# The first norm's rows stored unscaled, and scaled for the residual in the mLSTM, a block of rows at a time

## The chip, the cores and the metric

The kernel runs on one core of a Trainium2 chip. A core has five engines with instruction queues of their own, which meet only at semaphores: TensorE (PE in the profile, its weight loads PEld), VectorE (DVE), ScalarE (ACT), GpSimd (POOL) and SyncE (SP), which here only issues transfers. Each engine takes its instructions strictly in the order of its row. The metric is the device time of one execution in microseconds (us).

## The reference, cut

One layer of a decoder over 1024 tokens of width 1024:

```python
x = layer_norm(x, ln_in_g, ln_in_b)
h = x @ w_in                      # 7888 columns: gated DeltaNet, mLSTM, latent attention, gates
y_gdn, y_mlstm, y_mla = gated_deltanet(...), mlstm(...), latent_attention(...)
merged = sum(sigmoid(gate_b) * (y_b @ P_b) for b in branches)
x = layer_norm(ALPHA * x + merged @ w_out, ln1_g, ln1_b)      # ALPHA = 2 ** 0.25
x = layer_norm(ALPHA * x + routed_experts(x), ln2_g, ln2_b)
```

The change is about the term `ALPHA * x` of the second norm. With `xn` for the first norm's rows before their gain and shift, it is `xn * (ALPHA * ln_in_g) + ALPHA * ln_in_b`, row by row, 1024 rows of 1024 values.

## The kernel before

The 1024 rows are 8 blocks (`NB`) of 128 rows, a row to a partition. `input_norm` loads the rows into two tiles `xh` (four blocks each), normalises them in place on ScalarE and turns them through PE into `xH` and `xL`, the high and low part of x, with the gain and the shift put in on the way. So `xh` itself holds the rows without gain and shift. From then on PE works through `w_in` in chunks of 256 columns (tiles `wr` as loaded, `wh` and `wl` split). The first six wide chunks feed the convolutions of the gated DeltaNet: a product `psp`, its copy `ci` by ScalarE (`conv_half`, L519, after a small `memset` on GpSimd, L514), four taps `cy` on VectorE (L531, L533), a tanh on ScalarE, and `cth` to memory as `gqkv`. Beside them run the `gates_prep` steps (`da` on GpSimd, `c_mprev`, `c_mt` on VectorE, `c_emt` on ScalarE).

At the end of that stage `residual()` (L257) stores the residual: it zeroes one spare block of rows (`zr` to `x1r`), loads ALPHA times gain and shift into every partition (`gr`, `br`, L317, scaled on GpSimd in L319), and for each of the 8 blocks multiplies and adds on GpSimd (L265, L266) and stores `x0a` from GpSimd's own queue (L267). `out_proj` reads `x0a` much later.

PE's instruction order is written by hand for the whole front half. Independent products (`Filler`) are handed out in small pieces between dependent steps; the numbers `MRATE` and `MFILL` set how much of them stands between two steps. In the first stage GpSimd's order is by hand too; in the mLSTM the order on GpSimd, VectorE, ScalarE and SyncE is the scheduler's, but it is fixed at compile time.

The mLSTM (`mlstm`, L994) goes through the 8 blocks. `mlstm_prep` of block b+1 runs with `mlstm_main` of block b. A block's chain is: loads `mx`, `mv`, `mo_`; `mR` and its split on GpSimd and ScalarE (L914 to L919); PE's `mpk`, `mps`, `mpD`; an exponential into `mE` on ScalarE, masked on GpSimd (L931); `mkw`, `ms`, `mkk`, `mqd` on VectorE (L933 to L945); PE's `mpn` and `mpc`; on VectorE the denominators `mnn`, whose power of -1/2 is taken on GpSimd (L132, called from `rsqrt`); GpSimd scales `mo_` with it (L983); VectorE multiplies `mso` (L985); PE turns it (`mpy`), ScalarE copies it to `myT`, and SyncE stores it to `ym`. Meanwhile PE's filler computes the branch gates (`gt`, stored to `gates`).

Of the kernel before, what the change touches and what calls it, by code (L numbers as in the profile page):

```python
# [19 lines left out]
P = 128  # L20
# [124 lines left out]
class Filler:  # L145
    """Work for the tensor engine that waits for nothing, handed out in small pieces between dependent steps."""

# [27 lines left out]
def drive(k, us, *gens):  # L175
    """Steps the generators in turn, with filler after each step."""
    live = list(gens)
    while live:
        for g in list(live):
            try:  # L180
                n = next(g)
            except StopIteration:
                live.remove(g)
                continue
            k.fill.run(us * (n or 1.0))
# [8 lines left out]
def input_norm(k, late, todo, conv):  # L194
    """The first norm, a half of the rows at a time: while the first half is turned, the second is normalised. The
    tensor engine follows with the narrow columns of w_in, and the first wide ones' product with the first half."""
    nc, tc = k.nc, k.tc
# [59 lines left out]
    def residual():  # L257
        z = pool.tile([P, D], F32, name="zr", bufs=1)
        nc.gpsimd.memset(z, 0.0)
        nc.gpsimd.dma_start(k.x1r[T:T + P, :], z)  # L260
        gr = bcast_row(k, pool, k.ln_in_g, "gr", ALPHA)
        br = bcast_row(k, pool, k.ln_in_b, "br", ALPHA)
        for b in range(NB):
            xa = xh[b // 4][:, b % 4, :]
            nc.gpsimd.tensor_tensor(xa, xa, gr, OP.mult)  # L265
            nc.gpsimd.tensor_tensor(xa, xa, br, OP.add)  # L266
            nc.gpsimd.dma_start(k.x0a[b * P:(b + 1) * P, :], xa)  # L267

# [54 lines left out]
def load_raw(k, pool, src, segs, width, kt=KD, ncols=D_IN, tag="w", bufs=2, pieces=2, rtag=None, rbufs=2, rpool=None,  # L323
             now=False):
    """Loads a weight in pieces of its rows."""
    wh = pool.tile([P, kt, width], F32R, name=tag + "h", tag=tag + "h", bufs=bufs)
    wl = pool.tile([P, kt, width], F32R, name=tag + "l", tag=tag + "l", bufs=bufs)
    step = max(1, kt // pieces)

    def parts():  # L330
        for a in range(0, kt, step):
            n = min(step, kt - a)
            raw = (rpool or pool).tile([P, step, width], F32, name=tag + "r", tag=rtag or tag + "r", bufs=rbufs)
            o = 0
            for start, m in segs:
                ap = bass.AP(tensor=src.tensor, offset=src.offset + a * P * ncols + start,
                             ap=[[ncols, P], [P * ncols, n], [1, m]])
                k.nc.sync.dma_start(raw[:, :n, o:o + m], ap)
                o += m
            s = slice(a, a + n)  # L340
            yield raw[:, :n, :o], wh[:, s, :o], wl[:, s, :o]

    return wh, wl, list(parts()) if now else parts()


def split_raw(k, w):
    """Splits what was loaded into a high and a low part."""
    wh, wl, parts = w
    for raw, h, l in parts:
        k.nc.scalar.activation(h, raw, AF.Copy)  # L350
        k.nc.vector.tensor_sub(l, raw, h)  # L351
    return wh, wl
# [42 lines left out]
def chunks(k, todo):  # L395
    """Column chunks of w_in one after the other, each split one chunk ahead of its products."""
    def load(i):
        return load_split(k, k.wp, k.w_in, [(todo[i][0], 256)], 256)

    w = load(0)  # L400
    for i, (_, fn) in enumerate(todo):
        nxt = load(i + 1) if i + 1 < len(todo) else None
        yield from fn(w)
        w = nxt
# [117 lines left out]
def conv_steps(k, pool, t, ci):  # L522
    """The causal convolution of four taps over a row of columns, and its SiLU, operation by operation."""
    nc = k.nc
# [156 lines left out]
def inverse16(k, pool, b):  # L681
    """The 16-row diagonal blocks of the unit triangular inverse, row by row, a block to a partition."""
    nc = k.nc
# [14 lines left out]
    nc.sync.dma_start(blk_diag(k.gTd[b % 2]), X3)  # L698
    nc.sync.dma_start(blk_diag(k.gUd[b % 2]), t)


# [293 lines left out]
def mlstm(k):  # L995
    with k.tc.tile_pool(name="mls", bufs=1, side="right") as pool:
        Cn = pool.tile([P, H, P + 1], F32, name="mC")
        st = {}
        drive(k, k.rate, mlstm_prep(k, pool, 0, st))
        for b in range(NB):  # L1000
            gens = [mlstm_main(k, pool, b, Cn, st)]
            if b + 1 < NB:
                gens.insert(MORD, mlstm_prep(k, pool, b + 1, st))
            drive(k, MRATE, *gens)
            k.fill.run(MFILL)

# [52 lines left out]
def mla_prep(k, keep, lat, pool):  # L1059
    """The rotated keys and the normed latents, transposed."""  # L1060
    nc = k.nc
# [61 lines left out]
def mla(k, wn, wpool, after):  # L1123
    """Attention a head at a time: the scores of the next two blocks of rows go ahead of the values of these."""
    nc = k.nc
# [241 lines left out]
def route_choose(k, pool, lo, hi):  # L1367
    """Scores, choice and weights of the tokens of blocks lo to hi."""
    nc = k.nc
# [21 lines left out]
def route_place(k, pool, lo, hi):  # L1391
    """Places of the tokens of blocks lo to hi in their experts' rows, from 1; 0 where an expert is not chosen."""
    nc = k.nc
# [25 lines left out]
def route_weights(k, pool, lo, hi):  # L1419
    """The weights of the chosen experts, in three parts that add up exactly."""  # L1420
    nc = k.nc
# [22 lines left out]
def places(k, oh, aux, cols=(0, 6), parts=False):  # L1444
    """The rows of an expert's blocks: where to read, where to add, and their weights over the residual's scale. The
    first block has whole rows; of the others, with `parts`, each has 32 rows in quarters, partition 32q + r being
    quarter q of row r."""
    nc = k.nc
# [82 lines left out]
def mm_pair(k, outs, xH, xL, ws, first, last):  # L1531
    """One contraction step of two products that share their left operand."""
    for p in range(3):
# [14 lines left out]
class Weights:  # L1548
    """The experts' weights in the order of their use. A slot holds one as it comes, or the high or the low part of
    one; slots come free in a known order and are handed on in it."""  # L1550

# [44 lines left out]
    def step(self, split=True):  # L1596
        """After a step, the last to use the oldest parts."""
        self.free += self.parts.pop(self.done)[2:]
# [7 lines left out]
    def spare(self, keep=False):  # L1606
        """A slot for other data; with `keep`, one that outlives the experts."""
        i = next((i for i, (p, _) in enumerate(self.free) if p is not self.late), 0)
# [10 lines left out]
    def whole(self, keys):  # L1619
        """The weights as they come; each is asked for once."""  # L1620
        for key in keys:
            self.seen.add(self.index[key])
            yield self.raw[self.index[key]][0]
# [19 lines left out]
def experts(k, ws):  # L1643
    """Per expert a block of 128 rows always, and up to four of 32 rows each where it has more: those take a quarter of
    the columns in each quarter of the tensor engine. The tensor engine and the indirect transfers alone branch on the
    count: what the others read of a skipped product is finite and not added anywhere."""
    nc, tc = k.nc, k.tc
# [41 lines left out]
    with tc.tile_pool(name="moe", bufs=2) as pool:  # L1689
# [103 lines left out]
        def last_two(d, e):  # L1793
            """All but the rows of the last expert's first block goes into the residual first, and the last norm runs
            over all rows; then over those rows again, once they are whole."""
            a, norm = A[e], Norm(k)
# [73 lines left out]
def overflow(k):  # L1870
    """Rows past the first two blocks of an expert, added to the residual row by row, and the last norm over all rows
    again."""
    nc, tc = k.nc, k.tc
# [55 lines left out]
class Norm:  # L1929
    """The last norm: statistics on the scalar engine for some blocks, and the scale and shift on GpSimd for some."""  # L1930

# [25 lines left out]
    def rows(self, alloc):  # L1957
        """All rows, block by block: loads, statistics, scale, and the way out."""
        k, nc = self.k, self.k.nc
# [122 lines left out]
def out_proj(k, mH, mL, w, wA, xpool):  # L2082
    """The merged branches through w_out, a quarter of the columns at a time, and row by row the norm, the logits and
    the routing."""
    nc, tc = k.nc, k.tc
    with tc.tile_pool(name="wop", bufs=2) as pool:
# [63 lines left out]
        def logits(b):  # L2150
            """Four chunks at a time, each in a quarter of the tensor engine's columns."""
            pq = k.pb.tile([P, P], F32, name="plq", tag="t")
# [238 lines left out]
```

## Time and profile before

| what | value |
|---|---|
| median of 3 runs | 1935.11 us (1934.57, 1935.11, 1947.82) |
| span of the profiled execution | 1943.0 us |
| PE busy | 1735.4 us (89%) |
| DVE busy | 1225.7 us (63%) |
| ACT busy | 702.9 us (36%) |
| POOL busy | 601.7 us (31%) |
| mean granted TensorE clock | 0.950 |

The profile is of one execution. Its own time on the device beyond the span is not listed; the span alone lies between the second and the third of the runs. Times in a timeline are counted from the start of the span. A row of a timeline gives start, duration, engine, line, operation, output and inputs; what stands in brackets at the end is the idle time of the engine just before it and what ended that. Busy shares are means over stages that have different limits, so the stages are read one by one: the first norm and the convolutions up to about 220 us, the gated DeltaNet up to about 742, the mLSTM to about 877.

### The profile page before, as it was taken

What the parts mean: (1) busy time and instruction counts of PE and PEld (TensorE: products, weight loads), DVE (VectorE), ACT (ScalarE), POOL (GpSimd) and SP (SyncE); (2) the same over time, 40 slices, a digit from 0 to 9 for tenths busy, and PEclk for the clock granted to TensorE, in tenths of its full rate; (3) what the DMA queues carried; (4) which work ended last, traced back from release to release, by engine and by line L of the source; (5) the groups of instructions that cost most, each with busy time, mean ns of one, the idle gap of its engine ahead of it and who ended that gap; (6) DMA issues with size and microseconds to landing.
All of it is one profiled execution on the core that took longest, in us unless ns stands there. A gap on an engine that the chain in (4) does not pass through costs nothing. (4 is left out here: it accounts for less than half of the span.)

```text
span 1943.0 us, 29520 instructions
## 1 busy us (share of the span) xinstructions
PE 1735.4 (89%) x10830; PEld 1448.4 (75%) x10830; DVE 1225.7 (63%) x2279; ACT 702.9 (36%) x1166; POOL 601.7 (31%) x503
## 2 busy tenths in 40 slices
PE   6996999999999999999999899998488887788772
PEld 5974988899998888888777688897356655566551
DVE  7699654554555424444577657636776778899766
ACT  6311222212112213335344422212335455566453
POOL 3186021113301105531100200015434455455355
PEclk9998999999999999999999999998689998889886
DMA  5232633333332225432200365433557778788645
GB/s 170 88 109 108 186 101 119 96 104 112 102 107 80 94 78 163 137 123 104 62 18 29 124 195 181 163 114 142 209 186 222 236 229 267 233 283 299 206 116 201
DMA packets 210665, 286.42 MB, mean 147 GB/s; under 512 B 33358, under 2 KB 138824, under 8 KB 210472
## 3 DMA queue, kind: packets, MB, share of 16 engines
q1 hardware_dynamic: 202312, 258.87, 40.3%
q0 software_dynamic: 8160, 24.91, 5.4%
q8 instruction: 129, 2.11, 0.4%
q14 instruction: 64, 0.52, 0.1%
HBM read 214.64 MB, written 69.07 MB: 146 GB/s over the span
## 5 line engine op out<-in xcount | busy, mean ns | idle before, releaser
L365 PE MATMUL psp<-xH,wh 128*128 128x512 f32 x704 | 286.4, 407 | 18.0 <-ACT ci L519 18.0
L366 PE MATMUL psp<-xL,wh 128*128 128x512 f32 x704 | 276.0, 392 | 4.2 <-POOL ci L514 2.3
L367 PE MATMUL psp<-xH,wl 128*128 128x512 f32 x704 | 276.9, 393 | 0.0
L365 PEld LDWEIGHTS psp<-xH,wh 128*128 128x128 f32 x704 | 133.3, 189 | 43.7 <-ACT ci L519 19.3
L365 PE MATMUL psp<-wh,xH 128*128 128x256 f32 (+1 forms) x576 | 165.7, 288 | 0.0
L367 PE MATMUL psp<-wh,xL 128*128 128x256 f32 (+1 forms) x576 | 162.4, 282 | 0.0
L366 PE MATMUL psp<-wl,xH 128*128 128x256 f32 (+1 forms) x576 | 162.4, 282 | 0.0
L366 PEld LDWEIGHTS psp<-xL,wh 128*128 128x128 f32 x704 | 133.3, 189 | 31.9 <-POOL ci L514 2.7
L367 PEld LDWEIGHTS psp<-xH,wl 128*128 128x128 f32 x704 | 132.8, 189 | 29.4
L1535 PE MATMUL ph<-wl,xgH 128*128 128x512 f32 x274 | 94.8, 455 | 19.6 <-PEq L1656 8.7
L365 PEld LDWEIGHTS psp<-wh,xH 128*128 128x128 f32 x576 | 110.4, 192 | 0.2
L366 PEld LDWEIGHTS psp<-wl,xH 128*128 128x128 f32 x576 | 110.4, 192 | 0.1
L367 PEld LDWEIGHTS psp<-wh,xL 128*128 128x128 f32 x576 | 110.3, 191 | 0.0
L351 DVE TENSOR_TENSOR wl<-wr,wh 128x1024 fp32r<-128x1024 f32 (+1 forms) x62 | 81.8, 1339 | 41.9 <-ACT wh L350 29.9
L350 ACT ACTIVATE wh<-wr 128x1024 fp32r<-128x1024 f32 (+1 forms) x62 | 64.0, 1048 | 64.6 <-PE psp L366 40.7
L1535 PEld LDWEIGHTS ph<-wl,xgH 128*128 128x128 f32 x274 | 55.5, 215 | 36.5 <-issue 11.5
L365 PE MATMUL pbr<-yH,brh 128*128 128x512 f32 x192 | 76.0, 396 | 0.5 <-DMA brr<-in_w_br_gdn_dram 0.5
L366 PE MATMUL pbr<-yL,brh 128*128 128x512 f32 x192 | 76.4, 398 | 0.0
L367 PE MATMUL pbr<-yH,brl 128*128 128x512 f32 x192 | 76.0, 396 | 0.0
L365 PE MATMUL pwo<-woh,mH 128*128 128x256 f32 x256 | 75.9, 297 | 0.0
L366 PE MATMUL pwo<-wol,mH 128*128 128x256 f32 x256 | 74.3, 290 | 0.0
L367 PE MATMUL pwo<-woh,mL 128*128 128x256 f32 x256 | 74.2, 290 | 0.0
(844 smaller groups left out, 4442.5 us busy)
## 6 DMA issues: line engine op xcount, KB each, us to landing
wl<-in_moe_w_dram SPq DMA_DIRECT2D x126, 256.0 KB
wr<-in_w_in_dram SPq DMA_DIRECT2D x60, 512.0 KB
xs<-in_moe_w_dram SPq DMA_DIRECT2D x82, 256.0 KB
wl<-in_moe_w_dram SPq DMA_DIRECT2D x34, 512.0 KB
gates<-gt SPq DMA_DIRECT2D x24, 512.0 KB
mgt<-gates SPq DMA_DIRECT2D x48, 256.0 KB
we<-in_moe_w_dram SPq DMA_DIRECT2D x48, 256.0 KB
we<-in_moe_w_dram SPq DMA_DIRECT2D x18, 512.0 KB
```

Source lines behind the costliest of these rows:

```text
L350: k.nc.scalar.activation(h, raw, AF.Copy)
L351: k.nc.vector.tensor_sub(l, raw, h)
L365: k.nc.tensor.matmul(out, aH, bH, start=start, stop=False)
L366: k.nc.tensor.matmul(out, aH, bL, start=False, stop=False)
L367: k.nc.tensor.matmul(out, aL, bH, start=False, stop=stop)
L1535: k.nc.tensor.matmul(ps, xL if p == 2 else xH, wl if p == 1 else wh, start=first and p == 0, stop=last and p == 2)
```

## The change

Two parts. In the first stage the rows of `xh` are stored to `x0a` as they are, by SyncE, without any work on GpSimd; the zero rows are stored by SyncE too. In the mLSTM a new class `Residual` loads `gr` and `br` and scales them, and after the steps of each block b its method `block(b)` loads 128 rows of `x0a` into a tile `rx` (two buffers), multiplies and adds on GpSimd, and stores them back to the same place. The other lines of the diff only empty docstrings, so that line numbers move.

```diff
     def residual():
         z = pool.tile([P, D], F32, name="zr", bufs=1)
         nc.gpsimd.memset(z, 0.0)
-        nc.gpsimd.dma_start(k.x1r[T:T + P, :], z)
-        gr = bcast_row(k, pool, k.ln_in_g, "gr", ALPHA)
-        br = bcast_row(k, pool, k.ln_in_b, "br", ALPHA)
+        nc.sync.dma_start(k.x1r[T:T + P, :], z)
         for b in range(NB):
-            xa = xh[b // 4][:, b % 4, :]
-            nc.gpsimd.tensor_tensor(xa, xa, gr, OP.mult)
-            nc.gpsimd.tensor_tensor(xa, xa, br, OP.add)
-            nc.gpsimd.dma_start(k.x0a[b * P:(b + 1) * P, :], xa)
+            nc.sync.dma_start(k.x0a[b * P:(b + 1) * P, :], xh[b // 4][:, b % 4, :])
...
+class Residual:
+
+
+    def __init__(self, k, pool):
+        self.k, self.pool = k, pool
+        self.gr = bcast_row(k, pool, k.ln_in_g, "gr", ALPHA)
+        self.br = bcast_row(k, pool, k.ln_in_b, "br", ALPHA)
+
+    def block(self, b):
+        nc, rows = self.k.nc, self.k.x0a[b * P:(b + 1) * P, :]
+        x = self.pool.tile([P, D], F32, name="rx", bufs=2)
+        nc.sync.dma_start(x, rows)
+        nc.gpsimd.tensor_tensor(x, x, self.gr, OP.mult)
+        nc.gpsimd.tensor_tensor(x, x, self.br, OP.add)
+        nc.sync.dma_start(rows, x)
...
         Cn = pool.tile([P, H, P + 1], F32, name="mC")
+        res = Residual(k, pool)
         st = {}
...
             drive(k, MRATE, *gens)
+            res.block(b)
             k.fill.run(MFILL)
```

PE's and ScalarE's rows keep their order, VectorE's but for one weight split that comes ahead of a `mso`. GpSimd's and SyncE's rows change. In the rows below, numbers behind a name tell buffers apart, and the lines of the changed kernel are its own: L914 to L919 of before are L926 to L931, L931 is L943, L983 is L995.

GpSimd at the start of the mLSTM, before: the second block's addition into `mR` and the first block's `mE` follow each other closely.

```order
L916 TENSOR_TENSOR mR<-mR,mR_6706 128x512
L915 TENSOR_TENSOR mR_6859<-ident,c_nmt 128x512
L931 TENSOR_TENSOR mE<-mE,TU 128x512
L919 TENSOR_TENSOR mRL<-mR,mRH 128x512
L914 TENSOR_TENSOR mR<-TU,c_fp 128x512
```

The same place in the changed kernel:

```order
L928 TENSOR_TENSOR mR<-mR,mR_6690 128x512
L314 TENSOR_SCALAR gr<-gr 128x1024
L927 TENSOR_TENSOR mR_6848<-ident,c_nmt 128x512
L314 TENSOR_SCALAR br<-br 128x1024
L943 TENSOR_TENSOR mE<-mE,TU 128x512
L931 TENSOR_TENSOR mRL<-mR,mRH 128x512
L926 TENSOR_TENSOR mR<-TU,c_fp 128x512
```

The two scalings of gr and br have come ahead of the first `mE`.

GpSimd right behind that, before, down to the first block's `mo_` (`mnn` is the power, L132):

```order
L916 TENSOR_TENSOR mR<-mR,mR_6859 128x512
L915 TENSOR_TENSOR mR_7008<-ident,c_nmt 128x512
L908 MEMSET mv_6853 128x4
L132 TENSOR_TENSOR mnn<-mnn,nhalf 128x4
L983 TENSOR_TENSOR mo__6635<-mo__6635,mnn 128x512
```

And in the changed kernel:

```order
L928 TENSOR_TENSOR mR<-mR,mR_6848 128x512
L709 TENSOR_TENSOR rx<-rx,gr 128x1024
L927 TENSOR_TENSOR mR_7002<-ident,c_nmt 128x512
L710 TENSOR_TENSOR rx<-rx,br 128x1024
L920 MEMSET mv_6842 128x4
L709 TENSOR_TENSOR rx<-rx,gr 128x1024
L710 TENSOR_TENSOR rx<-rx,br 128x1024
L132 TENSOR_TENSOR mnn<-mnn,nhalf 128x4
L995 TENSOR_TENSOR mo__6619<-mo__6619,mnn 128x512
```

The four passes over the first two blocks of rows stand ahead of the first block's power and `mo_`. In the second block three passes stand ahead of the power and one between it and `mo_`; in the third, four ahead of both.

GpSimd from the third block's `mo_` on, before:

```order
L983 TENSOR_TENSOR mo__6856<-mo__6856,mnn 128x512
L931 TENSOR_TENSOR mE<-mE,TU 128x512
L919 TENSOR_TENSOR mRL<-mR,mRH 128x512
L914 TENSOR_TENSOR mR<-TU,c_fp 128x512
L916 TENSOR_TENSOR mR<-mR,mR_7316 128x512
```

And in the changed kernel:

```order
L995 TENSOR_TENSOR mo__6845<-mo__6845,mnn 128x512
L709 TENSOR_TENSOR rx<-rx,gr 128x1024
L710 TENSOR_TENSOR rx<-rx,br 128x1024
L709 TENSOR_TENSOR rx<-rx,gr 128x1024
L943 TENSOR_TENSOR mE<-mE,TU 128x512
L710 TENSOR_TENSOR rx<-rx,br 128x1024
L931 TENSOR_TENSOR mRL<-mR,mRH 128x512
```

Three of the last four passes have come ahead of the fourth block's `mE`, and the last one right behind it. After that GpSimd's row is as before.

## Rows read from the trace of the kernel before

**Rows 1.** Who waited for whom, PE alone, 90 to 230 us (the front stage): us in total, times, longest.

```profile
PE psp L365 <- ACT ci L519: 18.0, 3, 16.5
```

**Rows 2.** Who waited for whom, ScalarE (ACT), 120 to 200 us: us in total, times, longest.

```profile
ACT cth L536 <- DVE cy L533: 36.5, 4, 15.2
...
ACT c_emt L507 <- DVE c_mt L505: 18.6, 1, 18.6
```

**Rows 3.** Timeline of VectorE (DVE) at the front: start in us, us, line, operation, tiles, shapes, count (a row with x3 gives the sum of three).

```profile
135.14 2.15 DVE L502 TENSOR_TENSOR c_mprev<-c_mprev,ml 128x4 f32<-128x4 f32 x1
...
137.32 0.16 DVE L503 TENSOR_TENSOR c_mprev<-c_mprev,ml 128x4 f32<-128x4 f32 x1
...
155.18 2.88 DVE L531 TENSOR_SCALAR cy<-ci,par 128x1024 f32<-128x1024 f32 x1
...
186.53 0.75 DVE L531 TENSOR_SCALAR cy<-ci,par 128x1024 f32<-128x1024 f32 x1
...
187.38 3.93 DVE L533 SCALAR_TENSOR_TENSOR cy<-ci,par,cy 128x1024 f32<-128x1024 f32 x3
```

**Rows 4.** Timeline of GpSimd (POOL) at the front, same columns.

```profile
121.78 2.79 POOL L319 TENSOR_SCALAR gr<-gr 128x1024 f32<-128x1024 f32 x1
...
124.55 3.19 POOL L319 TENSOR_SCALAR br<-br 128x1024 f32<-128x1024 f32 x1
...
134.86 2.41 POOL L265 TENSOR_TENSOR xh<-xh,gr 128x1024 f32<-128x1024 f32 x1
```

**Rows 5.** The instructions on the tile `xh`, with GpSimd's: duration in ns (min/median/max), first and last start; then the time of their DMAs from issue to landing.

```profile
L265 POOL TENSOR_TENSOR xh<-xh,gr x8: 2351/2411/2928, 127.7 to 174.8; 128x1024 f32<-128x1024 f32 x8
...
L266 POOL TENSOR_TENSOR xh<-xh,br x8: 2337/2420/3282, 130.6 to 177.3; 128x1024 f32<-128x1024 f32 x8
...
DMA to landing us min/median/max: 2.9/3.0/3.0
```

**Rows 6.** Busy time by stretches of 4 us, PE alone: us, PE busy (number of matmuls), granted clock (1.00 is full), share of the DMA engines, GB/s.

```profile
164.00:168.00 4.00, 1.72 (x4) 0.50 0.00 0
...
168.00:172.00 4.00, 4.00 (x11) 0.50 0.67 262
...
176.00:180.00 4.00, 4.00 (x19) 1.00 0.25 79
```

**Rows 7.** Timeline of SyncE's DMA issues, at the front and in the mLSTM (with x4 the time from the first to the last of four).

```profile
30.91 23.86 SPq L338 DMA_DIRECT2D wr<-in_w_in_dram  x4
...
123.92 3.58 SPq L338 DMA_DIRECT2D wr<-in_w_in_dram  x2
...
765.09 0.32 SPq L911 DMA_DIRECT2D mo__6856<-mo  x1
...
771.20 0.37 SPq L905 DMA_DIRECT2D mx<-mqk  x1
```

**Rows 8.** Busy time by stretches in the mLSTM: us, PE, PEld, DVE, ACT and POOL busy (number), granted clock, DMA share, GB/s.

```profile
746.00:750.00 4.00, 4.00 (x21) 3.14 (x20) 0.00 (x0) 1.04 (x2) 3.88 (x5) 1.00 0.95 296
```

**Rows 9.** Who waited for whom, PE alone, 736 to 900 us (the mLSTM).

```profile
PE mpn L959 <- DVE ms L937: 1.2, 1, 1.2
...
PE mpy L678 <- DVE mso L985: 0.4, 1, 0.4
```

**Rows 10.** Timeline of GpSimd in the mLSTM.

```profile
751.68 1.30 POOL L916 TENSOR_TENSOR mR<-mR,mR 128x512 f32<-128x512 f32 x1
...
754.06 1.30 POOL L931 TENSOR_TENSOR mE<-mE,TU 128x512 f32<-128x512 f32 x1
...
761.89 1.02 POOL L132 TENSOR_TENSOR mnn<-mnn,nhalf 128x4 f32<-128x4 f32 x1 [1.19 <-DVE mnn L980]
...
769.30 1.29 POOL L919 TENSOR_TENSOR mRL<-mR,mRH 128x512 fp32r<-128x512 f32 x1 [2.00 <-ACT mRH L918]
...
773.47 1.04 POOL L915 TENSOR_TENSOR mR<-ident,c_nmt 128x512 f32<-128x512 f32 x1
...
778.45 1.04 POOL L983 TENSOR_TENSOR mo__6703<-mo__6703,mnn 128x512 f32<-128x512 f32 x1 [0.28 <-DVE mnn L982]
...
798.51 1.48 POOL L931 TENSOR_TENSOR mE<-mE,TU 128x512 f32<-128x512 f32 x1 [2.72 <-ACT mE L930]
```

**Rows 11.** Timeline of PE in the mLSTM: the products that wait for GpSimd's and VectorE's results, first to fourth block.

```profile
757.27 1.16 PE L959 MATMUL mpn<-mv,ms 128*128 128x129 f32 x8 [1.17 <-DVE ms L937]
...
766.44 0.60 PE L678 MATMUL mpy<-ident,mso 128*128 128x128 f32 x4
...
782.81 0.60 PE L678 MATMUL mpy<-ident,mso 128*128 128x128 f32 x4
...
799.14 0.60 PE L678 MATMUL mpy<-ident,mso 128*128 128x128 f32 x4
...
804.85 0.39 PE L958 MATMUL mpn<-mC,mqd 128*128 128x129 f32 x2
```

**Rows 12.** Timeline of VectorE in the mLSTM.

```profile
755.39 1.23 DVE L933 TENSOR_SCALAR mkw<-mE 128x4 f32<-128x4 f32 x1 [15.28 <-POOL mE L931]
...
756.53 0.68 DVE L937 SCALAR_TENSOR_TENSOR ms<-mps,mE 128x512 f32<-128x512 f32 x1
...
764.27 0.76 DVE L985 TENSOR_TENSOR mso<-mpn,mo__6635 128x256 f32<-128x256 f32 x2 [1.15 <-POOL mo__6635 L983]
```

**Rows 13.** The head of the page: the span of the profiled execution.

```profile
span 1943.0 us, 29520 instructions
```

## The prediction

> **What bounds the kernel now.** I first read where TensorE (PE) waits, since its instruction order is fixed by the program and every wait on it moves all that follows. In the stage where the residual rows are scaled, PE waited 18.0 us for ScalarE's copy `ci` of a convolution's input, 16.5 of them in one piece [rows 1]. Behind that, ScalarE itself sat in its queue for VectorE: 18.6 us for `c_mt` and 36.5 us for the convolution's sum `cy` [rows 2]. So VectorE ended last. Its own rows tell why: a `tensor_tensor` of 128x4 took 2.15 us beginning at 135.14, and its twin a moment later 0.16; a `tensor_scalar` of 128x1024 took 2.88 where 0.75 is normal [rows 3]. The long ones end where a GpSimd (POOL) pass over `xh` ends: 134.86 + 2.41 = 137.27 [rows 4]. The 16 passes of the residual (2.41 us each) [rows 5] thus hold VectorE, and through ScalarE they stop PE.
>
> **Removed at the front.** The 16 passes, two scalings and nine software DMA issues leave POOL's queue between 121.8 and 180.6 (177.3 + 3.28) [rows 4, 5]; the 18.0 us of waiting go with them. Unblocked, VectorE needs per convolution row about 0.75 + 3.93 + 1.2 = 5.9 us [rows 3], under the 48 x 0.21 = 10 us of PE's products for one, so I see nothing else that would end last there. [...] **Gain: 18.0 + 2.6 = 20.6 us.** Its low bound comes from the spread of the runs (below): 12.2.
>
> **Moved on SP at the front.** Eight plain stores of 512 KB now stand around the weight loads. The first pair of those is issued at 30.91 and the second waits for its buffers until about 54.8 [rows 7]; five stores of some 0.4 us of issue lie in that gap, so they are covered. Without it, their 2.6 MB at 296 GB/s [rows 8] would be 8.9 us. The zero rows' store waits for POOL's memset, which comes at the same time as before, ahead of a weight load that was issued only at 123.92 [rows 7]. I take 0.
>
> **Added in the mLSTM.** POOL works strictly in its row, and the order shown in the section on the change is the whole matter: the new passes stand ahead of short ones that PE waits for. PE's row is unchanged, and it had next to no slack there (1.2 us of waiting for `ms`, 0.4 for `mso`) [rows 9]. I walk POOL's row on the old clock with the old durations; gr and br cost 2.79 and 3.19 [rows 4], a pass 2.41 [rows 5].
>
> *First block.* The addition into `mR` ends at 751.68 + 1.30 = 752.98 [rows 10]. From there: scalings 6.0, `mR` 1.04, `mE` 1.30, `mRL` 1.29, `mR` 1.04, addition 1.30, `mR` 1.05, four passes 9.64, gaps 0.5. The power (`mnn`, L132) starts at 776.1 instead of 761.89 [rows 10]: 14.2 us late, and with it `mo_`, `mso` and PE's `mpy` (766.44 becomes 780.65) [rows 11]. Of that, 4.9 show already at `mpn`: `mE` ends at about 761.3, and with 0.2 for `mkw` and 0.68 for `ms` [rows 12] PE goes on at 762.2 instead of 757.27. **14.2.**
>
> *Second block.* `mRL` follows ScalarE as before, 2.86 us after `mpy`; the third `mR` then ends at 788.7 (773.47 + 1.04 was 8.07 after `mpy`) [rows 10, 11]. The load of the third block of rows stands on SP behind `mx`, which was issued 4.76 us after `mpy` [rows 7]: 785.4, plus 0.5 to the next issue and 3.0 to land [rows 5], so 788.9, or up to 1.8 later behind `mx`'s 512 KB; I take 789.8, 1.1 after POOL is free. Three passes precede the power and a fourth precedes `mo_`: 789.8 + 4 x 2.48 + 1.02 + 0.28 + 1.04, so 802.1, and `mso` lets `mpy` start at 803.0. PE would be there 16.37 after the last `mpy` [rows 11], at 797.0. **6.0.**
>
> *Third block.* The load of the fifth block waits for the store of the fourth, and that store stands on SP behind the load `mo_`, which waits for this `mso` (in the old run too) [rows 7, 12]. So it lands near 806.8. Then four passes 9.92, `mRL`, `mR` twice, an addition, power, `mo_`, `mso` together 7.9: `mpy` at 824.6 against 803.0 + 16.33 [rows 11]. **5.3.**
>
> *Fourth block.* Three passes stand ahead of `mE`, which before started 2.7 us after `mo_` [rows 10]: 823.8 + 7.44 + 1.4, so 832.6; a fourth pass starts just then and holds VectorE for 2.41; `mkw`, `ms`, `mkk`, `mqd` take 2.2. `mpn` at 837.3 against 824.6 + 5.71 [rows 11]. **7.0.** After that the rows are as before. That `mkw`, a `tensor_scalar` of 128x4, is held by a GpSimd operation is in the old trace: it took 1.23 us at 755.39, beside `mRL` [rows 12]. [...]
>
> **Cost: 32.5 us.** Low bound 25: the loads come in time and VectorE is not held (14.0, 4.6, 2.0, 4.5). High bound 40: VectorE held once more in two blocks (4.8) and a drop of the clock at the last stall (2.6). The loads of gr and br ahead of `mx` are 1 MB at 296 GB/s [rows 8], so `mx` comes 3.5 us later; POOL's 4.9 covers that, and without it the 3.5 would be the price. The later rows on SP (gates' store, weight loads) come up to 15 us later, but their buffers are used again only one or two blocks (16.37 us each [rows 11]) later. I take 0 for them, with 2 as the price of one miss.
>
> **Sum.** On the profiled execution, whose span is 1943.0 [rows 13]: 1943.0 - 20.6 + 32.5 = 1954.9. What lies around the span isn't shown. It is 7.9 above the median of 1935.11, and the runs spread from 1934.57 to 1947.82, so the stall at the front may well be shorter in the quicker ones (20.6 - 8.4 = 12.2, the low bound). Carrying the difference of +11.9 over to the median gives **1947.0**: the gain at the front is more than paid back in the mLSTM.
>
> **Rivals.**
> - *The passes are hidden in the mLSTM.* POOL waited there 1 to 3 us between its instructions [rows 10], and PE has other products to do. Then only the gain stays: 1935.1 - 20.6 = 1914.5. Against it: a pass takes 2.41 and four stand in one block, and PE's filler is fixed in its row. 7 in 100.
> - *Slower by over 1%, by the clock.* PE stands still four times for 5 to 9 us. After the long wait at the front its granted clock went to half, and running up again cost 2.6 [rows 6]. Should each stall do that and none of it overlap with POOL's lateness, 4 x 2.6 = 10.4 more: 1957.4. It decides where a stall is long enough for the clock to fall; the rows show only that 16.5 us was. [...] Against it: a PE that runs slowly while POOL is the late one loses little. 15 in 100.
> - *Slower by over 1%, by a smaller gain.* Where the quick runs had little of the front's stall (12.2), and the cost is at 35 to 40: 1935.1 - 12.2 + 37 = 1960. The spread of the runs speaks for it, the profile for the opposite. 15 in 100.
> - *The change doesn't free the front:* the `da` products ahead of the residual still run on POOL and hold VectorE, and another wait takes the place of the old one. With half of the stall left, +10: 1957. Nothing in the rows names such a wait. In the two cases above.
>
> **How the numbers follow.** Likeliest, 63 in 100: between +4.4 (20.6 against 25) and +19, so 1939 to 1954, value 1947.0. Slower by over 1% (above 1954.5) 30 in 100, faster by over 1% (below 1915.8) 7; about 1% is what a measurement of this kernel can tell from no change. The range runs from 1930, below the low bound of the sum in case a stall is half covered, to 1962, over both slower cases.
>
> **What would show it.** Right: no wait of PE for `ci` over 2 us at 120 to 170, and a `tensor_tensor` of 128x4 there at 0.16; in the mLSTM waits of PE for `ms`, `mso` or `mqd`, 25 to 40 us in all, over the first four blocks and none in the last four; POOL without a gap before the first `mnn`. [...]

## The result and the profile after

The changed kernel takes 1954.21 us (median of 14 runs, 1943.12 to 1960.23), the kernel before 1936.88 on the same chips (14 runs, 1930.57 to 1948.05). The ratio is 1.0083, 95% interval 1.0065 to 1.0101: a little under 1% slower. The forecast was 1947.0, in a range of 1930 to 1962.

**The front.** First, who waited for whom on PE from 90 to 230 us, in the changed kernel (us in total, times, longest); it answers to [rows 1]:

```profile
PE pkb L673 <- DVE gkb L757: 2.5, 1, 2.5
```

The wait for `ci` is gone; the one that is left belongs to the DeltaNet stage. VectorE's timeline there, against [rows 3], and PE's window from 130 to 170 (busy time and instructions of PE, its weight loads, VectorE, ScalarE, GpSimd, then the granted clock, DMA share and GB/s), against [rows 6]:

```profile
130.33 0.16 DVE L497 TENSOR_TENSOR c_mprev<-c_mprev,ml 128x4 f32<-128x4 f32 x1
...
134.16 0.75 DVE L526 TENSOR_SCALAR cy<-ci,par 128x1024 f32<-128x1024 f32 x1
...
135.01 3.92 DVE L528 SCALAR_TENSOR_TENSOR cy<-ci,par,cy 128x1024 f32<-128x1024 f32 x3
```

```profile
130.00:170.00 40.00, 40.00 (x178) 33.11 (x177) 26.77 (x41) 11.74 (x16) 0.31 (x3) 1.00 0.24 85
```

The small operations on `c_mprev` take 0.16 us, three of the convolution's steps 3.92 in a piece, and PE is busy for 40 of 40 us at a granted clock of 1.00.

**The mLSTM.** PE's waits from 700 to 900 us, against [rows 9]:

```profile
PE mpy L673 <- DVE mso L997: 17.1, 4, 7.8
PE mpn L970 <- DVE mqd L957: 6.2, 1, 6.2
PE mpk L673 <- DMA mx<-mqk: 5.6, 1, 5.6
```

With 0.2 at `mpD` these are 29.1 us of waiting, where it was 1.6 before. The products that waited, one by one, from PE's timelines (start, us, operation, and in brackets the idle time ahead of it), against [rows 11]:

```profile
733.19 1.09 PE L673 MATMUL mpk<-ident,mx 128*128 128x128 f32 x4 [5.60 <-DMA mx<-mqk]
...
741.25 1.06 PE L971 MATMUL mpn<-mv,ms 128*128 128x129 f32 x8
...
758.32 1.11 PE L673 MATMUL mpy<-ident,mso 128*128 128x128 f32 x4 [7.82 <-DVE mso L997]
```

```profile
782.20 1.12 PE L673 MATMUL mpy<-ident,mso 128*128 128x128 f32 x4 [4.67 <-DVE mso L997]
...
806.03 1.12 PE L673 MATMUL mpy<-ident,mso 128*128 128x128 f32 x4 [4.18 <-DVE mso L997]
...
820.82 0.77 PE L970 MATMUL mpn<-mC,mqd 128*128 128x129 f32 x2 [6.20 <-DVE mqd L957]
...
833.77 0.60 PE L673 MATMUL mpy<-ident,mso 128*128 128x128 f32 x4
```

Five waits between 733 and 821, and none at the fourth block's `mpy`. GpSimd's row says what it did meanwhile, against [rows 10]:

```profile
730.97 2.80 POOL L314 TENSOR_SCALAR gr<-gr 128x1024 f32<-128x1024 f32 x1
...
734.75 2.77 POOL L314 TENSOR_SCALAR br<-br 128x1024 f32<-128x1024 f32 x1
...
744.03 2.40 POOL L709 TENSOR_TENSOR rx<-rx,gr 128x1024 f32<-128x1024 f32 x1
...
747.39 2.40 POOL L710 TENSOR_TENSOR rx<-rx,br 128x1024 f32<-128x1024 f32 x1
...
749.78 2.35 POOL L709 TENSOR_TENSOR rx<-rx,gr 128x1024 f32<-128x1024 f32 x1
752.21 2.34 POOL L710 TENSOR_TENSOR rx<-rx,br 128x1024 f32<-128x1024 f32 x1
754.51 1.04 POOL L132 TENSOR_TENSOR mnn<-mnn,nhalf 128x4 f32<-128x4 f32 x1
...
769.87 2.40 POOL L709 TENSOR_TENSOR rx<-rx,gr 128x1024 f32<-128x1024 f32 x1 [3.14 <-DMA rx<-x0a]
...
788.91 2.40 POOL L709 TENSOR_TENSOR rx<-rx,gr 128x1024 f32<-128x1024 f32 x1 [6.00 <-DMA rx<-x0a]
...
807.31 2.37 POOL L709 TENSOR_TENSOR rx<-rx,gr 128x1024 f32<-128x1024 f32 x1 [1.79 <-DMA rx<-x0a]
...
816.52 2.34 POOL L710 TENSOR_TENSOR rx<-rx,br 128x1024 f32<-128x1024 f32 x1
```

The two scalings and four passes stand ahead of the first `mnn` (L132), which PE's `mpy` needs by way of `mo_` and `mso`. The sixteenth pass ends at 818.9: two blocks of rows were scaled with each of the first four mLSTM blocks, none with the last four. In the second, third and fourth of them GpSimd also stood idle until the next rows had been loaded (3.14, 6.00 and 1.79 us), and what stands behind the passes in its row waited with it. And PE's windows around the first long wait, with the granted clock in the last column but two:

```profile
746.00:750.00 4.00, 4.00 (x25) 3.47 (x24) 0.44 (x1) 2.12 (x6) 4.00 (x5) 1.00 0.06 17
750.00:754.00 4.00, 0.51 (x3) 0.07 (x1) 0.00 (x0) 0.00 (x0) 3.92 (x2) 0.97 0.33 131
754.00:758.00 4.00, 0.00 (x0) 0.00 (x0) 1.49 (x3) 0.00 (x0) 3.72 (x4) 0.50 0.66 262
758.00:762.00 4.00, 3.68 (x11) 3.06 (x12) 3.99 (x7) 2.15 (x6) 1.34 (x2) 0.50 0.55 182
762.00:766.00 4.00, 4.00 (x14) 3.16 (x14) 0.00 (x0) 0.69 (x1) 3.76 (x4) 0.75 1.02 293
766.00:770.00 4.00, 4.00 (x32) 3.75 (x30) 1.32 (x6) 0.71 (x2) 0.86 (x2) 1.00 0.85 309
```

PE stops at about 750.5, and when it goes on at 758.32 it does so at 0.50: 25 matmuls in the 8 us from 758 to 766, where 25 went into the 4 us from 746 to 750. So PE also worked more slowly behind this wait, at 0.50 until 762 and at 0.75 from there to 766; whether that adds to the time is taken up in the section on why the prediction came near.

### The profile page after: what moved, and what is told of

The parts are those of the page before. It is cut to its first block, busy times and chain, and to the rows that moved or that the text cites. A ratio compares the mean times of both kernels' runs of the same rounds, so it can differ in the third digit from the quotient of the medians.

```text
span 1951.9 us, 29525 instructions
## 1 busy us (share of the span) xinstructions
PE 1737.7 (89%) x10830; PEld 1454.4 (75%) x10830; DVE 1195.2 (61%) x2279; ACT 704.3 (36%) x1166; POOL 594.7 (30%) x494
## 5 line engine op out<-in xcount | busy, mean ns | idle before, releaser
L360 PEld LDWEIGHTS psp<-xH,wh 128*128 128x128 f32 x704 | 134.7, 191 | 25.1
L346 DVE TENSOR_TENSOR wl<-wr,wh 128x1024 fp32r<-128x1024 f32 (+1 forms) x62 | 77.5, 1268 | 52.9 <-ACT wh L345 40.9
```

The source lines that it names most:

```text
L360: k.nc.tensor.matmul(out, aH, bH, start=start, stop=False)
```

## The experiments

One place makes all of them comparable: PE's first `pqr`, the first product of the attention's queries, behind the mLSTM and the little stage after it. What varies later in the kernel doesn't touch its time. e1_front, f1_queue and o1_out add nothing to the mLSTM and should have it at the same time: it stands at 917.0, 917.0 and 915.2, so differences of less than 2 us at this place tell nothing. The total times need a caution. e1_front, f1_queue, e2_mlstm, e3_moves and e6_half compute another residual (gain and shift left out in whole or in part, or applied twice), so the rows can go to other experts. Behind the output projection's last transposes (`px`) PE runs 2806 matmuls before, in the changed kernel, in e1_front, f1_queue and e3_moves, but 2905 in e2_mlstm and 2707 in e6_half. The table gives the median, the ratio to the kernel before in the same series, PE's waits in the mLSTM (those for the positions behind it are left out) and that first `pqr`.

| kernel | us | ratio, 95% interval | PE's waits, us | first `pqr`, us |
|---|---|---|---|---|
| before | 1936.88 | | 1.6 | 937.4 |
| changed | 1954.21 | 1.0083 (1.0065 to 1.0101) | 29.1 | 955.7 |
| e1_front | 1913.13 | 0.9879 (0.9843 to 0.9914) | 1.5 | 917.0 |
| f1_queue | 1912.66 | 0.9861 (0.9812 to 0.9909) | 2.0 | 917.0 |
| e2_mlstm | 1990.02 | 1.0258 (1.0224 to 1.0292) | 31.9 | 979.4 |
| e3_moves | 1913.79 | 0.9883 (0.9849 to 0.9917) | 6.1 | 921.5 |
| e6_half | 1928.47 | 0.9937 (0.9913 to 0.9961) | 14.3 | 935.9 |
| m2_order | 1933.60 | 0.9975 (0.9952 to 0.9999) | 7.9 | 935.2 |
| m3_act | 1934.24 | 0.9967 (0.9944 to 0.9990) | 9.5 | 933.8 |
| e5_fill | 1955.64 | 1.0067 (1.0047 to 1.0087) | 17.4 | 948.6 |
| o1_out | 1933.33 | 0.9956 (0.9933 to 0.9979) | 1.7 | 915.2 |
| v1_vec | 1934.47 | 0.9980 (0.9959 to 1.0002) | 14.3 | 936.4 |
| v2_vec_later | 1929.22 | 0.9942 (0.9918 to 0.9966) | 8.4 | 927.7 |
| v3_vec_act | 1924.74 | 0.9920 (0.9888 to 0.9952) | 6.5 | 925.5 |

The theory after the result: the front gives what was forecast, GpSimd's passes stand in its row ahead of what PE waits for, and the granted clock of 0.50 behind each wait costs time besides (this last part doesn't hold as it stands, see the next section). Rivals: the gain at the front is smaller; the rows' DMAs do it; the passes cost by holding VectorE, wherever they stand.

**e1_front: the new front alone.**

```diff
-        res = Residual(k, pool)
...
-            res.block(b)
```

> The new front alone: rows go out unscaled through SyncE and are never scaled (the residual lacks the norm's gain and shift), and nothing is added to the mLSTM. If the gain is all at the front and is what the trace of the changed kernel shows (the mLSTM begins 22.0 us earlier), the time is 1936.9 - 22.0 = 1915 us. By the sum on record (20.6) it is 1916. If only the wait for the convolution's input goes and the clock is not regained (18.0), 1919. If part of the gain is given back behind the front or needs the passes' absence in the DeltaNet stage, 1920 to 1930.

0.9879 of before, 23.4 us by the ratio; at the first `pqr` 20.4 us earlier, at the first `mpk` 729.2 against 749.5. Within those 2 us the gain at the front is the 20.6 of the sum.

**f1_queue: that front with the stores still on GpSimd's queue.**

```diff
-        nc.sync.dma_start(k.x1r[T:T + P, :], z)
+        nc.gpsimd.dma_start(k.x1r[T:T + P, :], z)
...
-            nc.sync.dma_start(k.x0a[b * P:(b + 1) * P, :], xh[b // 4][:, b % 4, :])
+            nc.gpsimd.dma_start(k.x0a[b * P:(b + 1) * P, :], xh[b // 4][:, b % 4, :])
```

> The front without the passes, the rows stored unscaled, but from GpSimd's queue as before, and nothing in the mLSTM (the residual lacks gain and shift). If the front's gain is the passes' (the rows' stores moved to SyncE count for nothing, as the sum on record has it), it is that of e1_front: 1913 us, within 4. If stores on GpSimd's queue held up part of the front, 1918 to 1925.

The first `pqr` stands at 917.0 in both, and the medians are 1912.66 and 1913.13. Which queue stored the rows counted for nothing here; the passes and scalings were the stall.

**e2_mlstm: the new mLSTM behind the old front.**

```diff
-        nc.sync.dma_start(k.x1r[T:T + P, :], z)
+        nc.gpsimd.dma_start(k.x1r[T:T + P, :], z)
+        gr = bcast_row(k, pool, k.ln_in_g, "gr", ALPHA)
+        br = bcast_row(k, pool, k.ln_in_b, "br", ALPHA)
         for b in range(NB):
-            nc.sync.dma_start(k.x0a[b * P:(b + 1) * P, :], xh[b // 4][:, b % 4, :])
+            xa = xh[b // 4][:, b % 4, :]
+            nc.gpsimd.tensor_tensor(xa, xa, gr, OP.mult)
+            nc.gpsimd.tensor_tensor(xa, xa, br, OP.add)
+            nc.gpsimd.dma_start(k.x0a[b * P:(b + 1) * P, :], xa)
```

> The new part of the mLSTM alone: the front is that of the kernel before, and the mLSTM loads, scales and stores each block of rows once more (rows are scaled twice). If the mLSTM's waits and the half clock behind them are the whole cost (28.7 + 11.5 us in the trace of the changed kernel), 1936.9 + 40.2 = 1977 us. If half clock gives back what it takes later in the kernel, 1936.9 + 28.7 = 1966. By the sum on record (32.5), 1969. If the cost arises only together with the earlier mLSTM, under 1960.

PE's waits in its mLSTM:

```profile
PE mpy L678 <- DVE mso L1002: 19.7, 4, 7.8
PE mpn L975 <- DVE mqd L962: 7.3, 1, 7.3
PE mpk L678 <- DMA mx<-mqk: 4.9, 1, 4.9
```

At the first `pqr` it is 42.0 us behind before, of which 30.3 are new waits; the other 11.7 have no wait beside them. The total is 8 us more than that (13 over the forecast of 1977), and it is lost behind the start of the output projection (1280.7 against 1241.2). There this kernel has the 99 matmuls more that were named above, and from the last `px` to the end its trace takes 581.2 us against 571.3. That is the likely cause, not a shown one: the traces with 2806 matmuls alone spread from 558.7 to 573.2 us there.

**e3_moves: the DMAs without GpSimd's work.**

```diff
-        self.gr = bcast_row(k, pool, k.ln_in_g, "gr", ALPHA)
-        self.br = bcast_row(k, pool, k.ln_in_b, "br", ALPHA)
+        self.gr = bcast_row(k, pool, k.ln_in_g, "gr")
+        self.br = bcast_row(k, pool, k.ln_in_b, "br")
...
-        nc.gpsimd.tensor_tensor(x, x, self.gr, OP.mult)
-        nc.gpsimd.tensor_tensor(x, x, self.br, OP.add)
```

> The changed kernel without the sixteen passes and the two scalings by ALPHA on GpSimd (rows come in and go out of SBUF unscaled in the mLSTM, so the residual lacks gain and shift); all DMAs stay. If the passes' place in GpSimd's order is what costs, only the wait for mx behind the two rows of gain and shift stays (5.6 us and some 2 us of half clock): 1915 + 7.6 = 1923 us, and mpy waits under 1.5 us in the first four blocks. If the DMAs of the rows slow the mLSTM's own loads, 1935 or more, with waits for mx or mv.

One wait for `mx`, 5.7 us, and 4.5 us at the first `pqr` against e1_front; nothing else. The total, 9 us under the 1923 that I had expected, doesn't tell it from e1_front. The rows' 16 transfers of 512 KB are not the cost by themselves, and of the 38.7 us that the changed kernel lies behind e1_front, 34 come only with GpSimd's work. That includes GpSimd's own waits for the rows' loads (10.9 us in the changed kernel): here nothing on GpSimd stands behind those loads, so this run doesn't show what their landing late costs there.

**e6_half: eight passes in place of sixteen.**

```diff
-        nc.gpsimd.tensor_tensor(x, x, self.br, OP.add)
```

> The changed kernel with eight of the sixteen passes: the multiplications by the gain stay, the additions of the shift are left out (the residual lacks the shift). All DMAs stay. If the cost goes with GpSimd's time, half of the 34 us that the passes cost at the mLSTM's end (38.7 against the new front alone, less 4.5 for the wait for mx) is gone: 1914 + 17 = 1931 us. If GpSimd has slack for a pass or two a block and only the rest costs, under 1922. If a single pass ahead of mnn already costs as much by the clock, over 1940.

18.9 us behind e1_front at the first `pqr`, 14.4 without the 4.5 for `mx`: less than half of 34. The waits for `mso` are 8.4 in 4, the longest 4.6. Half the work costs somewhat under half; there is no large free allowance.

**m2_order: the same passes in another order.** GpSimd's order is taken from the program, and the generator of a block of rows is stepped with the mLSTM's, so that one pass follows `mo_` and one follows `mE`.

```diff
+        with tc.manual_schedule(engines={ENG.PE, ENG.Pool}):
-        mlstm(k)
+            mlstm(k)
...
-        res = Residual(k, pool)
...
         drive(k, k.rate, mlstm_prep(k, pool, 0, st))
+        res = Residual(k, pool)
...
+            gens.append(res.block(b - 1) if b else res.rows())
             drive(k, MRATE, *gens)
-            res.block(b)
...
+        drive(k, 0.0, res.block(NB - 1))
...
         nc.gpsimd.tensor_tensor(x, x, self.gr, OP.mult)
+        yield 0.001
```

> The changed kernel with GpSimd's order in the mLSTM written out by hand: one pass behind the output gate's product, one behind the mask's product, a block of rows with each block, none ahead of mnn; the two rows of gain and shift are loaded behind the first block's loads and scaled in the first block. The same passes and DMAs run, plus nothing. If the order on GpSimd is the cause, the mpy waits shrink from 16.7 us to under 5, mx's 5.6 are gone and the clock stays at 1.00: 1915 to 1925 us. If the passes cost by holding VectorE's operations or by their length wherever they stand, the waits move to mE, mRL or ms and the time is 1935 to 1955.

20.5 us of the 38.7 go, by the order (and the later loads of `gr` and `br`) alone: no wait for `mx`, none of over 0.4 us for `mso`. In this order GpSimd never waits for the load of a block of rows either, so those waits are part of the 20.5. What is left, PE's waits and VectorE's timeline of one block:

```profile
PE psr L1040 <- DVE posf L1034: 7.6, 1, 7.6
PE mpn L976 <- DVE mqd L963: 7.5, 4, 2.9
PE mpy L673 <- DVE mso L1003: 0.4, 1, 0.4
```

```profile
777.18 4.98 DVE L346 TENSOR_TENSOR wl<-wr,wh 128x1024 fp32r<-128x1024 f32 x2
782.08 2.40 DVE L951 TENSOR_SCALAR mkw<-mE 128x4 f32<-128x4 f32 x1
784.36 0.68 DVE L955 SCALAR_TENSOR_TENSOR ms<-mps,mE 128x512 f32<-128x512 f32 x1
...
785.56 1.44 DVE L963 TENSOR_TENSOR mqd<-mx,mw 128x512 f32<-128x512 f32 x1
```

```profile
776.43 2.41 POOL L714 TENSOR_TENSOR rx<-rx,gr 128x1024 f32<-128x1024 f32 x1
...
781.04 3.38 POOL L716 TENSOR_TENSOR rx<-rx,br 128x1024 f32<-128x1024 f32 x1
```

`mkw` is 128x4 and took 0.17 us in the changed kernel's unhindered blocks; beside a pass it took 2.40 here and ended with it (782.08 + 2.40 = 784.48, 781.04 + 3.38 = 784.42). So the second rival holds for this part: 7.5 us of waits for `mqd` come from VectorE being held. The 7.6 at `psr` come because the positions' load needs the memory of the last rows, whose store is late. The time, 1933.6, lies above the 1925 that I had expected for the order as the only cause.

**m3_act: the same, the scalings on ScalarE, one block of rows fewer at the end.**

```diff
+        for t in (self.gr, self.br):
+            k.nc.scalar.activation(t, t, AF.Copy, scale=ALPHA)
...
-            gens.append(res.block(b - 1) if b else res.rows())
+            gens.append(res.block(b))
...
-        drive(k, 0.0, res.block(NB - 1))
```

> GpSimd's order by hand as in the run m2_order, with the two rows of gain and shift scaled by ALPHA on ScalarE, so that each block of rows goes with its own block and only one is left behind the last. If the 7.6 us that PE waited for the rotary positions there came from the two blocks of rows behind the last mLSTM block, that wait falls by 4.8, and the time from 1933.6 to about 1928 us. If the waits for mqd (7.5 us in four blocks) are VectorE held by GpSimd's passes, they stay at 6 to 9 us. If neither holds, 1933 again.

`psr`'s wait fell by 2.9 us, to 4.7, those for `mqd` rose to 9.5, and the time is the same. A miss: only 1.4 us at the first `pqr`, which is within the 2 us that tell nothing.

**e5_fill: PE's waits filled with other products.**

```diff
-            drive(k, MRATE, *gens)
+            drive(k, MRATE + (2.5, 1.5, 1.5, 2.0, 0, 0, 0, 0)[b], *gens)
```

> The changed kernel with more of TensorE's free-standing work handed out after each step of the mLSTM's first four blocks (2.5, 1.5, 1.5 and 2.0 us more a step, some 30 us in all, taken from the work that is left for the stage behind). GpSimd's passes stay where they are. If PE's waits and the half clock behind them are the cost, the mpy and mqd waits of 22.9 us shrink below 8 and the granted clock stays near 1.00: 1954 - 15 - 8 = 1931 us, between 1922 and 1938. If the work is missed in the next stage, whose steps then wait, or if the later GpSimd steps fall behind by as much as PE's work moves up, 1945 to 1955.

The waits in the mLSTM fell to 17.4 us, and the first `pqr` came 7.1 us sooner. But the stage behind had lost its filler:

```profile
PE pct L1100 <- DVE cn L1094: 7.6, 4, 4.1
PE pqr L360 <- ACT uqrh L345: 5.4, 3, 3.7
PE pv__8521 L360 <- ACT ukvh L345: 2.2, 1, 2.2
```

The attention's first scores start at 989.0 against 990.3 in the changed kernel. The rival outcome came: the hole only moved.

**o1_out: the scaling in the output projection, in place.**

```diff
+                xa = xs[b][:, lo:lo + 256]
+                nc.gpsimd.tensor_tensor(xa, xa, gb1[0], OP.mult)
+                nc.gpsimd.tensor_tensor(xa, xa, gb1[1], OP.add)
```

> The new front, nothing added to the mLSTM: the rows are scaled and shifted in place, a quarter of the columns at a time, when they are loaded for the output projection (64 operations of 128x256 on GpSimd and eight small scalings). No second way through memory. GpSimd stands idle for 140 us ahead of that place in the trace of the changed kernel, and the projection's first two quarters don't use it. If GpSimd keeps up with PE there, 1913 plus 3 to 10 us = 1916 to 1923. If each addition on VectorE now waits for GpSimd's two operations (about 1.4 us a quarter by 2.40 us for 1024 columns, for 64 of them 45 us, beside parts of PE of some 3 us each), PE waits in that stage and the time is 1930 to 1945.

The mLSTM is as in e1_front, and the projection's products take from 1219.0 to 1357.8, 138.8 us in place of 125.7, with a new wait:

```profile
PE px L2173 <- DVE xs L2132: 11.3, 1, 11.3
```

GpSimd's idle 140 us lie ahead of the rows' loads there, not behind them. 1933.33: the second outcome.

**v1_vec, v2_vec_later, v3_vec_act: the passes on VectorE.** Each adds one edit to the one before: the engine; the rows `gr` and `br` behind the first block's loads; their scaling on ScalarE.

```diff
-        nc.gpsimd.tensor_tensor(x, x, self.gr, OP.mult)
-        nc.gpsimd.tensor_tensor(x, x, self.br, OP.add)
+        nc.vector.tensor_tensor(x, x, self.gr, OP.mult)
+        nc.vector.tensor_tensor(x, x, self.br, OP.add)
...
-        res = Residual(k, pool)
...
         drive(k, k.rate, mlstm_prep(k, pool, 0, st))
+        res = Residual(k, pool)
...
+        for t in (self.gr, self.br):
+            k.nc.scalar.activation(t, t, AF.Copy, scale=ALPHA)
```

> The changed kernel with the sixteen passes on VectorE in place of GpSimd, nothing else (the two scalings by ALPHA stay on GpSimd, ahead of the first block). VectorE's operations on 128x1024 took 1.2 to 1.5 us in the traces and it is busy 16 to 21 us of 40 in this stretch of the kernel before its change, so the passes are some 20 us beside 60 free ones. If GpSimd's pace and its place ahead of mnn and the gate's product are the cause, the mpy waits fall from 16.7 us to under 6; the 4.5 us by the wait for mx stay: 1914 + 4.5 + 3 to 8 = 1921 to 1927 us. If work of this length in front of the chain costs wherever it runs, VectorE being the chain's own engine, 1940 or more.

> As v1_vec, with the two rows of gain and shift loaded behind the first block's loads. The wait for mx (5.6 us in the trace of the changed kernel) goes with its 4.5 us at the mLSTM's end: 1917 to 1922 us, below v1_vec by 3 to 5 us. If the rows' loads were hidden behind something else that is late at this place, the same time as v1_vec.

> As v2_vec_later, with the two scalings by ALPHA on ScalarE, so that GpSimd has nothing new in the mLSTM. In v2_vec_later PE still waited 5.0 us for mso once, and GpSimd was busy all of the 20 us ahead of it, 5.6 of them with these two scalings. If that is the cause, the wait falls under 2 us with the half clock behind it: 1929 - 5 to 8 = 1921 to 1924 us. If VectorE's passes themselves are late there, 1927 to 1931.

The engine takes 19.3 us off the first `pqr` (955.7 to 936.4), but `mpy` still waited 9.2 us in v1_vec where I had expected under 6, and 1934.47 lies above the range I gave. The later loads take another 8.7, more than e3_moves' 4.5, but 1929.22 is 7 us over the range I gave for v2_vec_later: `mpy` still waits 8.0 us there, 5.0 of them in one piece. With the scalings on ScalarE that longest wait falls to 2.5 (I had expected under 2) and the first `pqr` comes 2.2 earlier, hardly more than the 2 us that tell nothing; 1924.74 lies between the two outcomes. In v3_vec_act, which computes all that the reference asks for, this is left:

```profile
PE mpy L673 <- DVE mso L999: 3.6, 3, 2.5
PE mpn L972 <- DVE mqd L959: 2.7, 1, 2.7
```

0.9920 of before, and 0.984 of the changed kernel (0.9920 / 1.0083). It beats both, by 0.5 to 1.1% against before.

## Why the prediction came near, step by step

- **The front's gain, 20.6:** right. The rows that were to show it do ([rows 1, 3, 6] and their answers), and e1_front gives 20.3 at the first `mpk`, 20.4 at the first `pqr`, 23.4 (16.7 to 30.4 by the interval) in all, on another residual. No run shows the sum's 2.6 of clock by itself. It is an estimate from [rows 6], 5.7 us for 15 products of 4.00 / 19 = 0.21 each at 1.00, and e1_front is 2.3 and 2.4 further ahead at those two places than the 18.0 of waiting. The low bound of 12.2 wasn't needed, nor the rival with a smaller gain. SP's stores at 0: f1_queue bears it out.
- **The place of the cost:** right. GpSimd's row holds the passes ahead of `mnn`, `mE` and `mo_`, and the waits stand in the first four blocks alone, but for 0.4 us at the last `mpy` that the kernel before has too. m2_order shows that the order makes about half of the cost, the earlier loads of `gr` and `br` included.
- **The first block, 14.2:** right. Without its wait, `mpk` would have started at 733.19 - 5.60 = 727.59; in e1_front `mpy` comes 745.72 - 729.2 = 16.5 after `mpk`, here 758.32 - 727.59 = 30.7, so 14.2. The part forecast at `mpn` (4.9) came at `mpk` instead (5.6), by the loads of `gr` and `br`; `mpn` then found its operands ready. "Covered" thus held while the scalings were there. Alone the loads cost 4.5 (e3_moves) where I put 3.5. Read by how late `mpy` comes against `mpk`, the cost would look like 8.6 (25.1 against e1_front's 16.5), since `mpk` itself was late.
- **The second to fourth blocks, 6.0, 5.3 and 7.0:** here is the mis-sized step. From `mpy` to `mpy` these blocks took 23.9, 23.8 and 27.7 us where e1_front has 16.4, 16.3 and 16.4: 7.5, 7.5 and 11.4 too long. The sum of the four is 40.6 in place of 32.5. The term that was too small is the landing of the rows' loads, put at 3.0 us from issue to landing by the rows of the front [rows 5]; in the changed kernel their median is 6.1. The table gives when GpSimd's passes began, counted from the `mpy` of the block before, and how long it took from there to the next product that waited (`mpy`, `mpy`, `mpn`), in us:

| block | begin, forecast | begin, measured | from there, forecast | from there, measured |
|---|---|---|---|---|
| second | 9.2 (789.8 - 780.65) | 11.5 (769.87 - 758.32) | 13.2 | 12.3 |
| third | 3.8 (806.8 - 803.0) | 6.7 (788.91 - 782.20) | 17.8 | 17.1 |
| fourth | -0.8 (823.8 - 824.6) | 1.3 (807.31 - 806.03) | 13.5 | 13.5 |

The passes began 2.4, 2.9 and 2.1 us late, and what follows in GpSimd's row took no longer than forecast. Together that is 5.8 of the missing 8.1. The first of these loads was issued earlier than forecast (762.47, 4.2 us after `mpy` in place of 5.3), so it is the landing that was late. The DMA engines were busy meanwhile (1.02 and 0.85 in the two windows shown from 762 to 770), but no run took the other transfers away, so why the loads landed late stays open.
- **The clock behind a wait:** the other 2.3. From the fourth block's `mpn` to the next `mpy` PE took 12.95 us (833.77 - 820.82) without a wait, where e1_front takes 10.66; the granted clock was 0.50 until 824 and 0.65 until 826. The high bound has 2.6 for just this, a drop at the last stall. The clock was at 0.50 behind the other waits too (the windows from 732 to 736, 758 to 762, 782 to 786 and 806 to 810). Of the 40.6, 28.5 are waits, and 0.8 of waiting that e1_front has at `mpn` is gone, so PE worked 12.9 us longer in all (11.7 in e2_mlstm). But behind the earlier waits PE next had to wait for GpSimd again, and in the second to fourth blocks GpSimd's row ran from the landed load to that point with no gap but 0.28 us for VectorE. By that a quicker PE would only have waited longer there. So the argument that "a PE that runs slowly while POOL is the late one loses little" fits the rows. That is read from the timelines; no run held the clock still.
- **The rival "slower by the clock"** (1957.4): the time, 1954.2, lies nearer to it than to 1947.0, but not by its mechanism. The clock fell at each stall, as it says, but of its 10.4 us the rows show only about 2.3 that nothing else covered. The 1954.2 also lies just above the stretch from 1939 to 1954 that I called likeliest.
- **VectorE held, in the fourth block's 7.0:** right. In the fourth block `mkw` took 2.29 us, until the pass of 816.52 had ended at 818.86, and `ms` behind it only 0.68:

```profile
816.60 2.29 DVE L945 TENSOR_SCALAR mkw<-mE 128x4 f32<-128x4 f32 x1 [5.84 <-POOL mE L943]
818.80 0.68 DVE L949 SCALAR_TENSOR_TENSOR ms<-mps,mE 128x512 f32<-128x512 f32 x1
```

- **The sum:** with the terms as measured at the mLSTM's end, -20.4 and +38.7, the change is +18.3, and the medians differ by 17.3; the forecast was +11.9.

## What to carry to other kernels

A pass that is moved to a "free" engine takes its place in that engine's row; ask which short operations stand behind it there and who waits for them, and look at the order that results, not at the loop in which it is written: here two blocks of rows went with each of the first four blocks, none with the last four. Where the moved work needs a load of its own, take the time of that load from loads of its size at its new place: the 3.0 us, a median of the stores at the front, became a median of 6.1 for the loads in the mLSTM (3.1 for the stores there), and what stood behind them in the row waited. Why the loads landed late was not shown. Add the slow clock behind a stall of PE only where nothing else is late at the next wait: here the 2.3 us behind the fourth block's `mpn`, at 0.50 until 824. Where work must go somewhere, a faster engine (here VectorE, a median of 1.22 us a pass in v2_vec_later where GpSimd took 2.40 in the changed kernel) may cost less than the idle one.

## What the runs showed of the hardware

- Which of VectorE's operations a pass on GpSimd holds. In m2_order `mkw` (a `tensor_scalar` on 128x4 in SBUF) took 2.3 to 2.4 us in six of eight blocks, until the pass had ended, and 0.17 in the unhindered blocks of the changed kernel. `ms` and `mkk`, which read PSUM and follow right behind it, never took more than 0.68 there, beside GpSimd's next operations on `mR`; `mqd`, with two inputs in SBUF, took 1.44 (its median), also beside an operation on `mR`, where its median in the changed kernel is 0.69. The longer time lies in the operations' own durations and not in a wait ahead of them. So for these rows it does not hold that the engines meet only at semaphores, as the section on the chip has it.
- Short waits and the clock. In m2_order PE waited up to 2.9 us four times between 740 and 860 us and the windows stayed at 1.00; in v3_vec_act a wait of 2.7 us that ended at 754.9 was followed by 0.69 from 756 to 760. Waits of 4.2 us and more were followed by 0.50 in the changed kernel each time. In m3_act, with four waits of up to 2.9 us, the granted clock was 1.00 from 740 to 820 and 0.98 from 820 to 860. So in these runs waits of nearly equal length went either way.
